# Half-width matmuls in a blocked triangular inverse, and an attention bias table written and read in small parts

## The chip, the cores and the metric

The kernel runs on one core of one Trainium2 chip. The metric is the device time of one execution in microseconds (us), lower is better. Beside the runs' times there is one execution recorded by the hardware profiler; all durations below come from that one.

## What is computed

Eleven stages work one after the other on a state of 256 tokens by 1024 columns: an RWKV-7 mixer, a gated embedding, a differential attention, a second gated embedding, a norm, a feed-forward, a Mamba-2 mixer, two more feed-forwards, a sliding attention, and a fourth feed-forward. Only two of them matter here. The RWKV mixer runs, per head, a recurrence over the tokens:

```python
def step(state, inp):
    r_t, w_t, k_t, v_t, kk_t, b_t = inp
    sa = jnp.einsum('bhij,bhj->bhi', state, kk_t)
    state = (state * w_t[:, :, None, :] - sa[..., None] * b_t[:, :, None, :]
             + v_t[..., None] * k_t[:, :, None, :])
    return state, jnp.einsum('bhij,bhj->bhi', state, r_t)
```

and the sliding attention adds to its scores a bias that depends on head and distance alone:

```python
dist = qi - kj                        # 128 queries, 256 keys
in_window = (dist >= 0) & (dist < 128)
bias = rel_bias[t5_bucket(dist)]      # 32 buckets x 16 heads
s = einsum('bqkrd,bskd->bkrqs', qk, kk) * scale + bias
s = jnp.where(in_window & ..., s, -inf)
```

A feed-forward is `h + 0.5 * ((silu(u @ w1) * (u @ w3)) @ w2)` with `u` the normed state, 1024 columns in and 2816 between.

## The kernel before, in words

**Weights.** Every large weight matrix is streamed in pieces of 512 KB (`wload`, L337). A piece is loaded by a DMA on SyncE's queue (SP) into a tile `wr` (L346), ScalarE (ACT) rounds it to the matmul's four-byte format into `wh` (L350, through the helper at L223), VectorE (DVE) writes the rounding's rest into `wl` (L351, through L198), and TensorE (PE) multiplies with both (L226). DMAs on SP go out in the order of its rows; each waits until its slot of `wr` has been read. In a feed-forward a block of 256 columns (`blocks`, in `ffn` at L510) takes four pieces, two of w1 and two of w3; there are eleven blocks, then the second half's 22 pieces with w2 (`halves`).

**The inverse levels.** The RWKV recurrence is solved in two chunks `t` of 128 tokens for four groups `g` of four heads. For each of these eight (t, g), `scores` (L800) needs the inverse of a unit triangular 128 x 128 matrix per head. It is built by doubling: in half precision, `xt` holds the inverse of the diagonal blocks of size b, `xx` its transpose, `dt` the matrix. A level `lv` from 1 to 6 (b = 2 to 64) joins blocks of size b to blocks of 2b with three products of 128 x 128 per head, four heads in one PSUM bank of 512 columns: `ps` = dt times xx, DVE multiplies it with the level's mask `lev[:, lv]` into `mp` (L849, tile tag `h`), then `pa` = mp times xt and `pb` = xt times mp, which ACT copies into a new `xt` and a new `xx`. A mask has ones on the diagonal too, so the old blocks come through the product. The last level has no `pb`, and ACT writes `X`, the inverse in the four-byte format, for `solve`. That is 12 matmuls per level and chain at levels 1 to 5, 8 at level 6; with the transposition ahead of the levels (4 matmuls, L841) 72 a chain. All `t16` tiles share 14 slots under the tag `h`.

**What sets the order.** The code is written as generators that `weave` advances in turn: four streams `stream(g)` start at steps 0, 9, 24 and 33 (`ST`), and within one the second chunk's `scores` starts five steps after the first's (`SH`). A level takes two steps (two `yield`). Beside them run the gate projections, the bias vector, the embedding's projections and the first output pieces. On top of that a tile scheduler reorders instructions within each engine and chooses the number of slots of a tag where it has room (the numbers in the code are its start); an instruction under `late` keeps its place.

**The bias.** `bias_vec` (L1361) runs within the RWKV stage: one matmul of the table `rel_bias` (33 rows with one for the window, 16 heads) with a one-hot matrix gives a vector of 384 values per head, and one DMA writes it 16 times over into `scr` in DRAM. At the end of the third feed-forward (`ffn10`), `load_bias` (L1376) reads it back with eight DMAs on GpSimd's queue (POOL), each 16 partitions wide, shifted by one element per query, which gives the table `bias`, 128 queries x 16 heads x 256 keys. The sliding attention that follows adds it to its scores.

Of the kernel before, what the change touches and what calls it, by code (L numbers as in the profile page):

```python
# [18 lines left out]
P = 128  # L19
# [20 lines left out]
def constants():  # L40
# [9 lines left out]
    for lv in range(7):  # L50
        b = 1 << lv
        m = (row // (2 * b) == col // (2 * b)) & (row // b % 2 == 0) & (col // b % 2 == 1)
        c[:, C_LEV + lv * P:C_LEV + (lv + 1) * P] = (m if lv == 0 else m.T) | (row == col)
# [32 lines left out]
def take(gen, n):  # L86
    for _ in range(n):
        next(gen)
        yield
# [52 lines left out]
class Net:  # L142
# [367 lines left out]
    def ffn(self, i, j, nxt, kv=False):  # L510
# [114 lines left out]
    def rwkv(self, nxt):  # L625
# [20 lines left out]
        lev = self.m([P, 8, P], F16, tag="lev", bufs=1)  # L646
        self.G.dma_start(lev[:, :7], self.cdram[:, C_LEV:C_LEV + 7 * P].rearrange("p (a b) -> p a b", a=7))
        i16 = lev[:, 7]
# [152 lines left out]
        def scores(t, g):  # L801
# [25 lines left out]
            dt, xt, xx = self.t16(), self.t16(), self.t16()  # L827
            self.add(v4(dt[:]), G[:, 0], bc4(self.ident))
            self.mul(v4(xt[:]), v4(dt[:]), bc4(lev[:, 0]))
# [12 lines left out]
            self.act(xx[:], ps[:])  # L842
            yield
            for lv in range(1, 7):
                ps = self.pq()
                for q in hs:
                    self.mm(ps[:, q], dt[:, q], xx[:, q])
                mp = self.t16()
                self.mul(v4(mp[:]), v4(ps[:]), bc4(lev[:, lv]))  # L849
                yield  # L850
                pa = self.pq()
                for q in hs:
                    self.mm(pa[:, q], mp[:, q], xt[:, q])
                if lv < 6:
                    pb = self.pq()
                    for q in hs:
                        self.mm(pb[:, q], xt[:, q], mp[:, q])
                    xt, xx = self.t16(), self.t16()
                    if True:
                        self.act(xt[:], pa[:])  # L860
                    else:
                        self.V.tensor_copy(xt[:], pa[:])
# [98 lines left out]
        self.V.tensor_copy(i16, self.ident)  # L961
# [623 lines left out]
```

## Time and profile before

| | |
|---|---|
| median of 3 runs | 1540.28 us (1538.38 to 1541.55) |
| profiled execution | 1541.87 us, its span 1540.1 us |
| mean granted PE clock | 0.995 of full speed |
| PE busy with matmuls | 1488.0 us, 97% of the span |
| PE busy with weight loads (beside matmuls) | 1260.3 us, 82% |
| DVE | 1134.3 us, 74% |
| ACT | 874.3 us, 57% |
| POOL | 80.3 us, 5% |
| moved by DMA | 246.98 MB, mean 160 GB/s |

The profiled execution is the one that the views of the trace describe; it took 1.6 us longer than the median. A busy share is a mean over all stages. In the views, a form as `128*128 128x512 f32` is the weights' size and the moved operand's; `LDWEIGHTS` (under PEld) is the load of weights into PE's array that stands ahead of each matmul. A duration of one matmul reaches from its start to its result's end, and matmuls overlap; how fast they follow is seen from starts or from a group's whole length.

### The profile page before, as it was taken

What the parts mean: (1) busy time and instruction counts of PE and PEld (TensorE: products, weight loads), DVE (VectorE), ACT (ScalarE), POOL (GpSimd) and SP (SyncE); (2) the same over time, 40 slices, a digit from 0 to 9 for tenths busy, and PEclk for the clock granted to TensorE, in tenths of its full rate; (3) what the DMA queues carried; (4) which work ended last, traced back from release to release, by engine and by line L of the source; (5) the groups of instructions that cost most, each with busy time, mean ns of one, the idle gap of its engine ahead of it and who ended that gap; (6) DMA issues with size and microseconds to landing.
All of it is one profiled execution on the core that took longest, in us unless ns stands there. A gap on an engine that the chain in (4) does not pass through costs nothing.

```text
span 1540.1 us, 23304 instructions
## 1 busy us (share of the span) xinstructions
PE 1488.0 (97%) x8756; PEld 1260.3 (82%) x8756; DVE 1134.3 (74%) x1958; ACT 874.3 (57%) x1534; POOL 80.3 (5%) x86
## 2 busy tenths in 40 slices
PE   4999999999999999999999999999999999999998
PEld 4988988777778888887887888888878887788887
DVE  6887887776687877559877678865868647777763
ACT  3546556464567655547666655554655545765552
POOL 0000001111201000000001000000100002000000
PEclk9999999999999999999999999999999999999999
DMA  7422333565446666555352656664796653356653
GB/s 210 140 81 59 90 91 131 191 198 154 151 136 193 199 188 190 190 180 149 112 151 84 216 156 189 191 215 140 171 240 191 208 189 110 96 172 185 188 181 109
DMA packets 185716, 246.98 MB, mean 160 GB/s; under 512 B 11017, under 2 KB 124713, under 8 KB 185604
## 3 DMA queue, kind: packets, MB, share of 16 engines
q1 hardware_dynamic: 179124, 233.87, 49.8%
q0 software_dynamic: 2720, 8.05, 2.3%
q10 hardware_dynamic: 3760, 3.58, 1.0%
q8 instruction: 69, 1.13, 0.3%
q14 instruction: 43, 0.35, 0.1%
HBM read 242.16 MB, written 3.54 MB: 160 GB/s over the span
## 4 chain that ended last, share of the span: by engine, by line
PE 84%; DVE 7%; DMA 3%; ACT 3%; POOL 2%; issue 1%; POOLq 0%; ACTq 0%; DVEq 0%
PE pl L226 69%; PE ps L226 12%; PE ps L229 3%; DVE wl L198 2%; DVE s L198 1%; DMA wr<-in_ffn_w_dram 1%; POOL m L234 1%; ACT s L223 1%; DVE s L210 1%; ACT wh L223 1%; DMA wa<-in_rw_a_dram 1%; POOL s L1015 1%; DMA wr<-in_rw_w_in_dram 1%; DVE ac L210 1%; ACT e L223 0%
## 5 line engine op out<-in xcount | busy, mean ns | idle before, releaser
L226 PE MATMUL pl<-wh,s 128*128 128x512 f32 (+1 forms) x2336 | 680.6, 370 | 1.1 <-ACT s L223 1.1
L198 DVE TENSOR_TENSOR wl<-wr,wh 128x1024 fp32r<-128x1024 f32 (+1 forms) x444 | 535.0, 1212 | 154.1 <-ACT wh L223 153.2
L223 ACT ACTIVATE wh<-wr 128x1024 fp32r<-128x1024 f32 (+1 forms) x444 | 458.2, 1043 | 125.6 <-PE pl L226 96.4
L226 PEld LDWEIGHTS pl<-wh,s 128*128 128x128 f32 x2336 | 423.4, 190 | 69.8 <-issue 3.0
L226 PE MATMUL pl<-s,wh 128*128 128x512 f32 x1344 | 472.1, 397 | 3.4 <-ACT wh L223 2.3
L226 PE MATMUL pl<-wl,s 128*128 128x512 f32 (+1 forms) x1168 | 430.6, 369 | 3.1 <-DVE wl L198 3.1
L226 PE MATMUL pl<-s,wl 128*128 128x256 f32 x1344 | 373.9, 279 | 1.3 <-DVE wl L198 1.3
L226 PEld LDWEIGHTS pl<-s,wh 128*128 128x128 f32 x1344 | 252.7, 188 | 63.3 <-ACT wh L223 2.6
L226 PEld LDWEIGHTS pl<-s,wl 128*128 128x128 f32 x1344 | 253.6, 189 | 2.5 <-DVE wl L198 1.8
L226 PEld LDWEIGHTS pl<-wl,s 128*128 128x128 f32 x1168 | 221.9, 190 | 37.8 <-DVE wl L198 4.7
L223 ACT ACTIVATE s<-pl 128x256 f32<-128x256 f32 (+1 forms) x184 | 73.3, 403 | 106.6 <-PE pl L226 102.0
L223 ACT ACTIVATE s<-s 128x512 fp32r<-128x512 f32 (+2 forms) x97 | 61.2, 631 | 87.3 <-DVE s L198 86.7
L198 DVE TENSOR_TENSOR s<-pl,s 128x256 f32<-128x256 f32 x168 | 70.3, 421 | 45.4 <-ACT s L223 45.3
L234 POOL TENSOR_TENSOR m<-m,base 128x2 f32<-128x2 f32 (+2 forms) x25 | 25.2, 1010 | 956.6 <-DVE m L215 934.9
L198 DVE TENSOR_TENSOR s<-s,s 128x512 fp32r<-128x512 f32 (+2 forms) x97 | 66.4, 685 | 1.5
L223 ACT ACTIVATE h<-ps 128x512 f16<-128x512 f32 x88 | 48.3, 600 | 32.8 <-PE ps L226 29.5
L223 ACT ACTIVATE s<-ps,base 128x256 fp32r<-128x256 f32 (+1 forms) x104 | 46.4, 471 | 32.3 <-DVE s L210 17.0
L223 ACT ACTIVATE junk<-H 128x512 bf16<-128x512 f32 x40 | 25.1, 627 | 45.3 <-DVE H L210 28.9
L210 DVE SCALAR_TENSOR_TENSOR s<-ps,base,s 128x256 fp32r<-128x256 f32 x96 | 43.9, 479 | 7.8 <-ACT s L223 7.0
L210 DVE SCALAR_TENSOR_TENSOR H<-pl,m,H 128x512 f32<-128x512 f32 x16 | 12.0, 751 | 47.1 <-PE pl L226 47.1
L226 PE MATMUL ps<-h,h 128*128 128x128 f16 x544 | 44.4, 220 | 2.1 <-ACT h L223 1.9
L210 DVE SCALAR_TENSOR_TENSOR s<-s,s 128x512 f32<-128x512 f32 x56 | 38.4, 686 | 10.6 <-ACT s L223 10.5
(235 smaller groups left out, 1385.8 us busy)
## 6 DMA issues: line engine op xcount, KB each, us to landing
wr<-in_ffn_w_dram SPq DMA_DIRECT2D x264, 512.0 KB, 4.1
wr<-in_ssm_w_in_dram SPq DMA_DIRECT2D x40, 512.0 KB, 4.6
wr<-in_rw_w_in_dram SPq DMA_DIRECT2D x32, 512.0 KB, 3.9
wr<-in_da_w_in_dram SPq DMA_DIRECT2D x32, 512.0 KB, 4.4
wr<-in_pe_w_gate_dram SPq DMA_DIRECT2D x16, 512.0 KB, 6.2
wr<-in_ssm_w_out_dram SPq DMA_DIRECT2D x16, 512.0 KB, 3.7
wr<-in_rw_w_out_dram SPq DMA_DIRECT2D x8, 512.0 KB, 6.5
wr<-in_da_w_out_dram SPq DMA_DIRECT2D x8, 512.0 KB, 6.8
```

Source lines behind the costliest of these rows:

```text
L198: return self.V.tensor_tensor(out=out, in0=a, in1=b, op=op)
L210: self.V.scalar_tensor_tensor(out=out, in0=a, scalar=sc, in1=b, op0=op0, op1=op1, **k)
L223: return self.A.activation(out, a, f, **k)
L226: self.T.matmul(out, l, r, start=start, stop=stop)
L229: self.T.transpose(out, a, self.ident)
L234: self.G.tensor_tensor(out=out, in0=out, in1=self.mhalf[:, :out.free_size()].rearrange("p (a b) -> p a b", a=out.shape[1]) if len(out.shap ...
L1015: self.G.tensor_tensor(out=a[:], in0=a[:], in1=b[:], op=ALU.add)
```

## The change

**Levels.** The masks of a level touch only the off-diagonal part: of the 128 columns of a head, `ps` matters in the 64 whose block is even, `pa` changes the 64 whose block is odd, `pb` the 64 that are even. So each product now moves 64 columns of a head in place of 128, cut out of the old tiles by the view `part(ap, lv, odd)`, whose 64 columns are blocks of b elements with b between. The four heads' 64 columns lie together in 256 columns of PSUM; `pa` and `pb` share one bank. `xt` and `xx` are updated in place: ACT writes only the changed 64 columns a head. `dt`, `xt` and `xx` of a chain are now one tile `inv` (four slots). The mask product goes into one fixed tile per level, `MP[lv]`, six tiles inside `lev`, which grows from 8 to 29 blocks of 128 columns; their other columns hold the identity for good, written once near the start by six POOL copies. The last level copies the unchanged half of `X` too, one ACT operation more. The masks in DRAM shrink to 64 columns for levels 1 to 6, so `lev`'s load is 4 blocks in place of 7.

**Bias.** `bias_vec` runs in the first feed-forward (`ffn00`). Its matmul gives 128 rows (each head eight times over) in place of 16, and `scr` holds each head 128 times in place of 16: eight DMAs on SP of 2 x 128 rows of 1.5 KB (384 KB), one per block from the third block on. `load_bias` in `ffn10` is eight DMAs on SP, each all 128 partitions of two heads (256 KB), one per block from the third on.

```diff
+        if lv == 0:
+            c[:, C_LEV:C_LEV + P] = m | (row == col)
+        else:
+            c[:, C_LEV + P + (lv - 1) * 64:C_LEV + P + lv * 64] = (m.T | (row == col))[:, i // b % 2 == 0]
...
+        bias = self.load_bias() if kv else self.bias_vec() if not (i or j) else iter(())
         for n0 in range(256, 2816, 256):
             l1, l3 = blocks(n0)
-            weave(chain(l1, l3), side) if n0 == 256 else weave(chain(l1, l3))
-        if kv:
-            self.load_bias()
+            weave(chain(l1, l3), side if n0 == 256 else spread(1, 6, take(bias, 1)))
+        weave(bias)
...
-        lev = self.m([P, 8, P], F16, tag="lev", bufs=1)
+        lev = self.m([P, 29, P], F16, tag="lev", bufs=1)
...
+        MP = {lv: lev[:, 1 + 4 * lv:5 + 4 * lv].rearrange("p a b -> p (a b)") for lv in range(1, 7)}
+        def part(ap, lv, odd):
+            return ap.rearrange("p (n two b) -> p n two b", two=2, b=1 << lv)[:, :, odd]
...
-            dt, xt, xx = self.t16(), self.t16(), self.t16()
+            three = self.m([P, 3, 512], F16, "inv", 4)
+            dt, xt, xx = three[:, 0], three[:, 1], three[:, 2]
...
             for lv in range(1, 7):
+                n, b = 256 >> lv, 1 << lv
+                c4 = lambda ap: ap.rearrange("p (n b) -> p n b", n=n)
+                cut = lambda x, q, odd: part(x, lv, odd)[:, q * n // 4:(q + 1) * n // 4]
                 ps = self.pq()
-                for q in hs:
-                    self.mm(ps[:, q], dt[:, q], xx[:, q])
-                mp = self.t16()
-                self.mul(v4(mp[:]), v4(ps[:]), bc4(lev[:, lv]))
+                for q in range(4):
+                    self.mm(ps[:, q * 64:(q + 1) * 64], dt[:, hs[q]], cut(xx, q, 0))
+                mp = MP[lv]
+                self.mul(h4(part(mp, lv, 0)), h4(c4(ps[:, :256])), levc[:, lv - 1]...broadcast_to([P, 4, n // 4, b]))
                 yield
                 pa = self.pq()
-                for q in hs:
-                    self.mm(pa[:, q], mp[:, q], xt[:, q])
+                for q in range(4):
+                    self.mm(pa[:, q * 64:(q + 1) * 64], mp[:, hs[q]], cut(xt, q, 1))
                 if lv < 6:
-                    pb = self.pq()
-                    for q in hs:
-                        self.mm(pb[:, q], xt[:, q], mp[:, q])
-                    xt, xx = self.t16(), self.t16()
-                        self.act(xt[:], pa[:])
-                    self.act(xx[:], pb[:])
+                    for q in range(4):
+                        self.mm(pa[:, 256 + q * 64:256 + (q + 1) * 64], xt[:, hs[q]], cut(mp, q, 0))
+                    self.act(part(xt, lv, 1), c4(pa[:, :256]))
+                    self.act(part(xx, lv, 0), c4(pa[:, 256:]))
                 else:
                     x = XT[t, g] = self.m([P, 512], F32R, "XT", 4)
-                    self.act(x[:], pa[:])
+                    self.act(part(x[:], lv, 0), part(xt, lv, 0))
+                    self.act(part(x[:], lv, 1), c4(pa[:, :256]))
...
+        for mp in MP.values():
+            self.late(self.G.tensor_copy(mp..., i16.unsqueeze(1).broadcast_to([P, 4, P])))
...
-              after(FP, chain(self.bias_vec(), self.ple_proj(0), self.ple_proj(1))), ...
+              after(FP, chain(self.ple_proj(0), self.ple_proj(1))), ...
...
     def bias_vec(self):
-        self.mm(ps[:16, :384], lh, oh[:33, :384])
-        self.scr = self.dp.tile([16, 16, 384], F32, tag="scr", name="scr")
-        self.G.dma_start(self.scr[:], vec[:16, :384].unsqueeze(1).broadcast_to([16, 16, 384]))
-        yield
+        self.mm(ps[:, :384], lh[:33, :P], oh[:33, :384])
+        self.scr = self.dp.tile([16, P, 384], F32, tag="scr", name="scr")
+        scr = self.scr[:].rearrange("h (c j) n -> (h c) j n", j=16)
+        for q in range(0, 16, 2):
+            yield
+            self.late(self.nc.sync.dma_start(scr[:, q:q + 2], vec[:, :384].unsqueeze(1).broadcast_to([P, 2, 384])))
...
     def load_bias(self):
-        for q in range(0, P, 16):
-            self.late(self.G.dma_start(self.bias[q:q + 16], ... ap=[[383, 16], [384 * 16, 16], [1, 256]]))
+        for h in range(0, 16, n):
+            yield
+            self.late(self.nc.sync.dma_start(self.bias[:, h:h + n], ... ap=[[383, P], [384 * P, n], [1, 256]]))
```

In the levels PE has as many instructions as before, and they are narrower. In the middle of a burst of level products on PE stood before (`h` are the half-precision tiles, `ps` a PSUM bank):

```order
L226 LDWEIGHTS h_983
L226 MATMUL ps_1011<-h_937,h_983 128x128
L226 LDWEIGHTS h_937
L226 MATMUL ps_1016<-h_983,h_937 128x128
L226 LDWEIGHTS h_937
```

and now stand (`inv` is a chain's tile of three, `lev` the tile with the masks and mask products):

```order
L231 LDWEIGHTS lev_95
L231 MATMUL ps_1014<-inv_942,lev_95 128x64
L231 LDWEIGHTS inv_942
L231 MATMUL ps_1014<-lev_95,inv_942 128x64
L231 LDWEIGHTS inv_942
```

The moved operand is 64 columns wide, each matmul still has its own load of weights, and both products go to one bank.

On SP in the first feed-forward a row of weight loads stood before:

```order
L346 DMA wr_6106<-in_ffn_w_2_dram 128x4x256
L346 DMA wr_6128<-in_ffn_w_2_dram 128x4x256
L346 DMA wr_6163<-in_ffn_w_2_dram 128x4x256
L346 DMA wr_6185<-in_ffn_w_2_dram 128x4x256
L346 DMA wr_6217<-in_ffn_w_2_dram 128x4x256
```

and now the writes of the bias vector stand between them:

```order
L351 DMA wr_5960<-in_ffn_w_2_dram 128x4x256
L1395 DMA scr<-s_5783 128x2x384
L351 DMA wr_5995<-in_ffn_w_2_dram 128x4x256
L1395 DMA scr<-s_5783 128x2x384
L351 DMA wr_6018<-in_ffn_w_2_dram 128x4x256
L351 DMA wr_6050<-in_ffn_w_2_dram 128x4x256
L351 DMA wr_6072<-in_ffn_w_2_dram 128x4x256
L351 DMA wr_6107<-in_ffn_w_2_dram 128x4x256
L1395 DMA scr<-s_5783 128x2x384
```

One write goes out ahead of about every fourth weight load from there on.

The bias table was read by eight rows on POOL, after the last of the third feed-forward's norm operations there:

```order
L234 TENSOR_TENSOR m_11485<-m_11485,base_72 128x2
L234 TENSOR_TENSOR m_11498<-m_11498,base_72 128x2
L1380 DMA bias<-scr 16x16x256 x8
L234 TENSOR_TENSOR m_13043<-m_13043,base_72 128x2
L1406 TENSOR_TENSOR m_13057<-m_13057,base_72 128x8 x2
```

and now by eight on SP, among that stage's weight loads:

```order
L351 DMA wr_11532<-in_ffn_w_2_dram 128x4x256
L1403 DMA bias<-scr 128x2x256
L351 DMA wr_11555<-in_ffn_w_2_dram 128x4x256
L351 DMA wr_11587<-in_ffn_w_2_dram 128x4x256
L351 DMA wr_11609<-in_ffn_w_2_dram 128x4x256
L351 DMA wr_11644<-in_ffn_w_2_dram 128x4x256
L1403 DMA bias<-scr 128x2x256
```

A read of two heads goes out ahead of about every fourth weight load, and the row with all eight is gone from POOL.

The built programs also differ in the slots of the weight tiles, of which the diff says nothing: `wr`, `wh` and `wl` lie at 6, 8 and 6 addresses before and at 3 each now. `wload`'s own numbers (3 and 3) are unchanged.

## Rows read from the trace of the kernel before

**Rows 1.** Page, busy time of each engine over the span (share), x instructions.

```profile
PE 1488.0 (97%) x8756; PEld 1260.3 (82%) x8756; DVE 1134.3 (74%) x1958; ACT 874.3 (57%) x1534; POOL 80.3 (5%) x86
```

**Rows 2.** Stretches (us): PE, PEld, DVE, ACT, POOL busy (instructions), granted clock, DMA share, GB/s.

```profile
100.00:250.00 150.00, 147.01 (x1423) 131.30 (x1422) 121.85 (x238) 86.80 (x158) 10.44 (x11) 1.00 0.30 84
500.00:640.00 140.00, 140.00 (x779) 121.34 (x778) 109.57 (x150) 82.62 (x124) 0.69 (x1) 1.00 0.66 197
```

**Rows 3.** Tile h (levels), duration ns min/median/max, first and last start us, forms.

```profile
L226 PE MATMUL ps<-h,h x544: 216/219/234, 100.3 to 274.3; 128*128 128x128 f16 x182
L226 PEld LDWEIGHTS <-h x576: 95/98/153, 99.2 to 274.3; 128*128 128x128 f16 x192
L223 ACT ACTIVATE h<-ps x88: 581/597/641, 99.6 to 265.8; 128x512 f16<-128x512 f32 x88
L198 DVE TENSOR_TENSOR h<-ps,lev x48: 672/683/693, 100.9 to 273.0; 128x512 f16<-128x512 f32 x48
```

**Rows 4.** Timeline, inverse levels: start us, us, engine line op tiles xcount [idle before <-releaser].

```profile
169.55 0.61 PE L226 MATMUL ps<-h,h 128*128 128x128 f16 x8
223.65 0.11 PEld L226 LDWEIGHTS <-h 128*128 128x128 f16 x2 [1.00 <-DVE h L198]
178.28 1.00 PE L226 MATMUL ps<-sa,GB 128*128 128x64 f32 x8
```

**Rows 5.** Tile bias, landing of its eight reads; waits 1095 to 1140 us: total, times, longest.

```profile
DMA to landing us min/median/max: 8.2/13.8/18.7
ACT wh L223 <- DMA wr<-in_ffn_w_dram: 9.2, 1, 9.2
```

**Rows 6.** Third feed-forward: PE's timeline, then the stretch 1125 to 1135 us.

```profile
1128.06 0.49 PE L226 MATMUL pl<-s,wh 128*128 128x512 f32 x1 [2.25 <-ACT wh L223]
1129.32 0.39 PE L226 MATMUL pl<-s,wl 128*128 128x256 f32 x1 [0.76 <-DVE wl L198]
...
1129.96 0.63 PE L226 MATMUL pl<-s,wh 128*128 128x512 f32 x1
...
1130.60 0.63 PE L226 MATMUL pl<-s,wh 128*128 128x512 f32 x1
...
1133.54 0.40 PE L226 MATMUL pl<-s,wh 128*128 128x512 f32 x1
...
1133.89 0.39 PE L226 MATMUL pl<-s,wh 128*128 128x512 f32 x1
...
1125.00:1135.00 10.00, 6.98 (x30) 5.56 (x30) 6.92 (x10) 6.64 (x11) 0.00 (x0) 0.83 1.10 336
```

**Rows 7.** Page, costliest groups, 256 columns out of PSUM: busy, mean ns | idle before, releaser.

```profile
L223 ACT ACTIVATE s<-pl 128x256 f32<-128x256 f32 (+1 forms) x184 | 73.3, 403 | 106.6 <-PE pl L226 102.0
L198 DVE TENSOR_TENSOR s<-pl,s 128x256 f32<-128x256 f32 x168 | 70.3, 421 | 45.4 <-ACT s L223 45.3
```

**Rows 8.** POOL's copies' neighbours: a group of lines; waits 20 to 100 us.

```profile
L1015 POOL TENSOR_TENSOR s<-s,s 128x512 f32<-128x512 f32 x8 | 14.0, 1756 | 51.5 <-DVE s L198 47.6 <-PE ps L229 3.9
POOL s L283 <- PE pl L226: 40.9, 1, 40.9
PE ps L226 <- DMA wa<-in_rw_a_dram: 5.6, 1, 5.6
```

**Rows 9.** Timeline of PE: the bias vector's matmul.

```profile
218.00 0.81 PE L226 MATMUL ps<-s,s 33*16 33x384 f32 x2
```

**Rows 10.** First feed-forward: one weight load's timeline; issues 500 to 640 us, median us to landing.

```profile
575.27 0.37 SPq L346 DMA_DIRECT2D wr<-in_ffn_w_dram  x1
588.77 1.05 ACT L223 ACTIVATE wh<-wr 128x1024 fp32r<-128x1024 f32 x1
590.67 1.22 DVE L198 TENSOR_TENSOR wl<-wr,wh 128x1024 fp32r<-128x1024 f32 x1
591.91 0.37 SPq L346 DMA_DIRECT2D wr<-in_ffn_w_dram  x1
wr<-in_ffn_w_dram SPq DMA_DIRECT2D x53, 512.0 KB, 4.4
```

More of the change, by code (lines that the diff above doesn't have):

```diff
@@ L87, in take @@
     for _ in range(n):
-        next(gen)
+        if next(gen, gen) is gen:
+            return
         yield
@@ L826, in scores @@
                 yield
-            dt, xt, xx = self.t16(), self.t16(), self.t16()
-            self.add(v4(dt[:]), G[:, 0], bc4(self.ident))
-            self.mul(v4(xt[:]), v4(dt[:]), bc4(lev[:, 0]))
+            three = self.m([P, 3, 512], F16, "inv", 4)
+            dt, xt, xx = three[:, 0], three[:, 1], three[:, 2]
+            self.add(v4(dt), G[:, 0], bc4(self.ident))
+            self.mul(v4(xt), v4(dt), bc4(lev[:, 0]))
             pv = self.pq()
@@ L961, in rwkv @@
         self.V.tensor_copy(i16, self.ident)
+        for mp in MP.values():
+            self.late(self.G.tensor_copy(mp.rearrange("p (h c) -> p h c", h=4), i16.unsqueeze(1).broadcast_to([P, 4, P])))
         weave(chain(*[value(g) for g in range(4)]), chain(lora(), mix(1, *xk), mix(0, *xr)))
@@ L973, in rwkv @@
         weave(after(FH, residual()), after(FG[0], spaced(FG[1], *[gate(g) for g in range(4)])),
-              after(FP, chain(self.bias_vec(), self.ple_proj(0), self.ple_proj(1))), when(done(OP[0]), after(OP[1], chain(take(l0, OP[2]), take(l1, OP[3])))),
+              after(FP, chain(self.ple_proj(0), self.ple_proj(1))), when(done(OP[0]), after(OP[1], chain(take(l0, OP[2]), take(l1, OP[3])))),
               *[after(n, stream(g)) for g, n in enumerate(ST)])
@@ L1361, in bias_vec @@
     def bias_vec(self):
[L1363 to L1365 removed]
+        l0, lh = self.s(), self.s()
+        self.late(self.V.memset(lh[:33, :P], 1.0))
+        self.G.dma_start(l0[:32, :16], self.I["rel_bias_2"])
+        self.V.tensor_copy(lh[:32, :P].rearrange("p (h c) -> p h c", c=8), l0[:32, :16].unsqueeze(2).broadcast_to([32, 16, 8]))
         oh = self.s()
[L1367 removed]
+        self.late(self.G.dma_start(oh[:33, :384], self.cdram[:33, C_OH:C_OH + 384]))
         ps = self.pq()
[L1369 removed]
+        self.mm(ps[:, :384], lh[:33, :P], oh[:33, :384])
         vec = self.s()
[L1371 to L1381 removed]
+        self.V.tensor_copy(vec[:, :384], ps[:, :384])
+        self.scr = self.dp.tile([16, P, 384], F32, tag="scr", name="scr")
[3 more added lines that the diff above has]
+            self.late(self.nc.sync.dma_start(scr[:, q:q + 2], vec[:, :384].unsqueeze(1).broadcast_to([P, 2, 384])))
+    def load_bias(self):
+        self.bias, n = self.cp.tile([P, 16, 256], F32, tag="bias", name="bias"), 2
+        for h in range(0, 16, n):
+            yield
+            a = self.scr[h]
+            self.late(self.nc.sync.dma_start(self.bias[:, h:h + n], bass.AP(tensor=a.tensor, offset=a.offset + 127,
+                                                                           ap=[[383, P], [384 * P, n], [1, 256]])))
     def swa(self, nxt):
@@ L1518, in run @@
             weave(self.ple_proj(0), self.ple_proj(1))
-            weave(self.bias_vec())
             if "diff" not in stages:
```

22 lines of the change are left out of this document (7 added, 15 removed).

## The prediction

> **What bounds the kernel now.** I read the busy table first: the reader is to see that TensorE (PE) is busy 97% of the span [rows 1], so time is to be had only where PE waits, where its clock is low, or where it has less to do. The stretches come next: from 100 to 250 us, where the inverse levels run, PE is busy 147.01 of 150 us at full clock, DVE 121.85 and ACT 86.80; in the first feed-forward, 500 to 640 us, PE is busy all 140.00 us and the DMA engines 0.66 of the time [rows 2]. So in the inverse stage the bound is PE's own work, with 3.0 us of waits; in the feed-forward it is PE alone. Third, the tile view of the levels, for what is halved [rows 3]; fourth, the timeline at single bursts, for how closely half-precision matmuls follow each other [rows 4]. Fifth, the waits and the timeline of the third feed-forward, the one stretch where a DMA stops PE [rows 5, 6].
>
> **Term 1, the levels on PE.** The count stays: 544 half-precision matmuls, each with its weight load [rows 3]. Each streams 64 columns where it streamed 128. Eight of them in a row take 0.61 us and one takes 0.219, so they start (0.61 - 0.22) / 7 = 56 ns apart [rows 3, 4]. No row has a half-precision matmul of 64 columns. From below: half the columns, half the distance, 28 ns. From above: nothing is gained, 56 ns, because each still loads 128 columns of weights; the row that speaks for this has four-byte weights and 64 columns, eight in 1.00 us, over 100 ns apart however few the columns [rows 4]. But the half-precision load is another thing: after a wait, two of them take 0.11 us together where one takes 0.098, so the second began within 15 ns of the first [rows 3, 4]. A load that lets the next begin after 15 ns is hidden behind 28 ns of columns. I take 30 ns: 544 x 26 = 14.1 us less PE work; bounds 0 and 15.2.
>
> A rule of the Trainium skill speaks against this term. Its page TensorE: Matmul & The Clock Gate, section LDWEIGHTS, prices a weight load by its columns, 128 / 1.2 GHz or 107 ns, and its section on the back-to-back gap gives about 81 ns for a pair with 128 columns; by that price halving the moved columns would give nothing. The rows with 56 ns a pair disagree with both figures.
>
> How much of it arrives? PE runs in order, so what a step of the inverse waits for must be covered by other PE work. That cover shrinks by 12 x 26 ns = 0.3 us per level and chain, with two or three chains interleaved. The wait shrinks as well: DVE's product from 683 to about 421 ns, each of two ACT evacuations from 597 to about 403, the durations of the same engines on 256 columns out of PSUM [rows 3, 7]: 0.26 + 0.39 = 0.65 us per level. About even, so I keep the 3.0 us of waits and add 2 for places where the cover was thin: **-12 us**. DVE and ACT lose 48 x 0.26 = 12.6 and 80 x 0.19 = 15 us of work, worth nothing by themselves, as neither is the bound. The extra copy of the last level on ACT, eight of about 0.4 us, ends in front of a chain's solve and is inside the 2 us. The mask products now go into one tile per level in place of a fresh one, so a second chain at the same level would wait; chains start five steps or more apart and a level is two steps, so I give it nothing (0 to +3).
>
> **Term 2, the copies at the start.** Six copies of identities on POOL. The nearest row is a POOL operation of 512 four-byte columns, 1.76 us, so at most 10.5 us; POOL then sat idle for 40.9 us, and PE itself waits 5.6 us there for its first small weights, wa [rows 8]. The copies stand behind the issue of those weights on POOL. Nothing; without that cover it would delay the column loads behind them, needed much later.
>
> **Term 3, the bias vector.** Its matmul, 0.81 us on PE [rows 9], leaves the inverse stage and comes back in the first feed-forward, where PE is as full: zero, 0.8 us either way. Its two small loads are issued by POOL, which is idle in that stretch, well before the matmul's place, so PE does not wait for them.
>
> **Term 4, the bias table.** Before, eight reads of 256 KB come at once on POOL's queue and take 8.2 to 18.7 us to land; in that time a weight load is late and ACT waits 9.2 us for it [rows 5]. PE's share of this is 2.25 + 0.76 us of waits, and then a stretch at the lower clock: over 1125 to 1135 us the granted clock is 0.83 of 2.4 GHz, which is (1 - 0.83) x 10 / 0.5 = 3.4 us at 1.2 GHz, behind those waits [rows 6]. The pairs of matmuls at 1129.96 and 1130.60 start 0.64 us apart, those at 1133.54 and 1133.89, back at 2.4 GHz, 0.35 [rows 6], so 3.4 x (1 - 0.35 / 0.64) = 1.5 us of it are lost. Spread over eight blocks of 11 us, a read of 256 KB stands before every fourth weight load; a weight load is twice that and is taken in 2.77 us at a DMA share of 0.66 [rows 2, 10], 1.8 us of DMA time, so a read costs 0.9. The share goes to about 0.74. PE is not stopped: **-4.5 us** (bounds 0 and -4.5).
>
> **Term 5, the writes.** Eight writes of 384 KB on SP's queue in the first feed-forward, each in front of every fourth weight load: 384 / 512 x 1.8 = 1.4 us each, share to about 0.78. The weights land 4.4 us after their issue [rows 10]. They hide if the weights are early enough. If that cover were gone, 8 x 1.4 = 11 us here and 8 x 0.9 = 7 in the third feed-forward would show.
>
> **Term 6, the weights' slots.** This the diff does not say. In the built program the three weight tiles lie at 3 addresses each, before at 6, 8 and 6. The row of a load issued at 575.27 and of its low half's end, 590.67 + 1.22 = 591.89, with the next issue into that slot at 591.91, shows six loads in flight, 16.6 us or 2.77 us each [rows 10]. With three slots a load must land, be rounded by ACT and be subtracted by DVE within 3 x 2.77 = 8.3 us. It needs 4.4 + 1.05 + 1.22 = 6.7 [rows 10]; in turn, with the evacuations between on ACT and DVE, the span from ACT's start at 588.77 to 591.89 is 3.1, which makes 7.5. So it fits, with 0.8 to 1.6 us to spare, and a slot comes free two loads, 5.5 us, before PE's next turn at it, of which 2.3 to 3.1 go to ACT and DVE: what is ready stands 2.4 to 3.2 us before PE wants it. A write of 1.4 us in front of every fourth load fits into the two together. But at stage borders, where ACT and DVE are held up, less is in stock. From bounds 0 and +6 (twelve borders at half a microsecond) I take **+2 us**.
>
> **Sum.** -12 - 4.5 + 2 = -14.5 us. The profiled execution took 1541.87 us, 1540.1 of it its span: 1527.4. The median of the runs, 1540.28, is 1.6 us lower than that execution; carried over, **1526 us**. A measurement of this kernel can tell about 0.2%, 3.1 us, from no change.
>
> **Rivals.**
> - **The weight load bounds the half-size matmul.** Pairs stay near 56 ns. For it: the four-byte row. Against it: the 15 ns. Then term 1 keeps only what shorter evacuations give to the 3.0 us of waits, say 1.5: -1.5 - 4.5 + 2 = -4, 1536. The page's load price ends here too. Chance 0.12.
> - **The chains become the bound.** PE's work shrinks but its in-order waits on DVE, ACT and the shared mask tiles grow: of 14 us 4 arrive, 1534. For it: PE already waits 3.0 us there, and work memory has become tighter for other tiles too. Against it: the wait shrinks with the cover. Chance 0.12.
> - **Slower: three slots are the bound.** Issue to the end of the low half takes more than 8.3 us; from that point on every load of the feed-forwards is paced by it. At 8.7 us a load takes 2.90 in place of 2.77 us, and 264 of them give +34 us: 1560. For it: 0.8 us to spare is little, and the transfers now stand between. Against it: the landing of 4.4 us was measured with six in flight, with fewer it is hardly longer. Chance 0.08.
> - **The transfers show.** The slots hold, but a load behind a write or read is late to PE: +11 to +18, most of the gain, 1541. Chance 0.06.
>
> **How the numbers follow.** The forecast keeps 0.62 and the predicted time is its own. Its own range is 1517 (all 15.2, no waits, -4.5, nothing for the slots) to 1532. With the first two rivals the range goes to 1538; what is left out above is 0.14, below a little. Faster by over 0.2% means under 1537.2: the forecast, the chains, and most of the first rival (its 1536 lies near the border): 0.82. The rest of that rival and the transfers make 0.10, the slots 0.08.
>
> **What would show it.** Right: half-precision matmuls of 64 columns about 30 ns apart; PE's waits from 100 to 240 us near 5 us; the first projection's start after the inverse some 12 us earlier; no wait and no stretch at 1.2 GHz in the third feed-forward; PE busy throughout the first one. In the slots, the distance from issue to the low half's end falls from 16.6 to 8.3 us. Wrong: a pair still at 56 ns; PE waiting for wh or wl inside a feed-forward; a stage after the inverse that takes longer than before by more than a microsecond or two.

## The result and the profile after

The changed kernel takes 1528.62 us (median of 13 runs, 1524.03 to 1536.37) where the kernel before, on the same chip, takes 1539.48 (13 runs): ratio 0.993, 95% interval 0.9913 to 0.9947, 10.9 us faster (8 to 13). The prediction was 1526, within 1517 to 1538, which is 14.3 us less than the 1540.28 it started from (ratio 0.9907). That ratio lies just outside the interval here and inside that of a later measurement on another chip (0.9883 to 0.9925). The recorded execution of the changed kernel takes 1528.67 us, its span 1526.9, 13.2 less than before's.

What answers to [rows 1], the page of the changed kernel:

```profile
PE 1474.7 (97%) x8756; PEld 1246.5 (82%) x8756; DVE 1125.5 (74%) x1959; ACT 859.7 (56%) x1542; POOL 80.6 (5%) x83
```

PE has lost 13.3 us of busy time and its share is the same, so over the whole span it waits as long as before (52 us). To [rows 3] answer these, from the views of the tiles `lev` and `inv` (min/median/max in ns, first and last start, forms):

```profile
L231 PE MATMUL ps<-inv,lev x192: 191/193/207, 103.2 to 259.6; 128*128 128x64 f16 x192
L203 DVE TENSOR_TENSOR lev<-ps,lev x48: 408/418/426, 102.0 to 258.5; 128x256 f16<-128x256 f32 x48
...
L228 ACT ACTIVATE inv<-ps x88: 365/385/629, 100.8 to 250.9; 128x256 f16<-128x256 f32 x80, 128x512 f16<-128x512 f32 x8
```

and to the bursts of [rows 4] these rows of PE's timeline (start us, us, engine, line, operation, tiles, count):

```profile
140.19 0.28 PE L231 MATMUL ps<-inv,lev 128*128 128x64 f16 x4
140.30 0.28 PE L231 MATMUL ps<-lev,inv 128*128 128x64 f16 x4
140.42 0.28 PE L231 MATMUL ps<-inv,lev 128*128 128x64 f16 x4
```

A group of four starts every 0.11 to 0.12 us, so the matmuls are 29 ns apart, against 56 before. In the stretches of [rows 2], and in the third feed-forward while the bias table is read (columns as there):

```profile
100.00:236.00 136.00, 132.81 (x1423) 120.02 (x1424) 110.96 (x238) 73.23 (x164) 8.81 (x8) 1.00 0.29 86
500.00:640.00 140.00, 140.00 (x758) 120.73 (x758) 102.87 (x137) 76.71 (x116) 0.00 (x0) 1.00 0.68 212
1095.00:1185.00 90.00, 89.88 (x521) 78.43 (x520) 72.70 (x103) 51.48 (x82) 1.54 (x1) 1.00 0.69 214
```

The first row is the same number of matmuls as in [rows 2] (1423) in 14 us less, with 3.2 us of waits where there were 3.0. The second is the first feed-forward with its writes, and PE does not wait. In the third row the waits of [rows 6] are gone. The weight load of [rows 10] is now, again in the first feed-forward:

```profile
566.44 0.37 SPq L351 DMA_DIRECT2D wr<-in_ffn_w_dram  x1
572.41 1.06 ACT L228 ACTIVATE wh<-wr 128x1024 fp32r<-128x1024 f32 x1 [1.44 <-issue]
573.50 1.23 DVE L203 TENSOR_TENSOR wl<-wr,wh 128x1024 fp32r<-128x1024 f32 x1 [0.48 <-ACT wh L228]
```

From issue to the low half's end it takes 574.73 - 566.44 = 8.3 us, three loads of 2.77 us, where it was 16.6.

To see where the time went, count PE's matmuls from the last one back: most are the same work in each kernel. The table has the time between the same marks (the 8300th, 6500th, 5500th, 4450th, 3560th, 2400th, 2000th and 960th from the end); in brackets what PE sat idle and how long it ran at 1.2 GHz, both in us. "Again" is a second recorded execution of the changed kernel; the last three are experiments that follow.

| stretch | before | after | after, again | levels alone | wide, spread | levels, tight |
|---|---|---|---|---|---|---|
| start to the levels | 88.4 (21.8, 6.8) | 89.5 (21.8, 0) | 88.2 (21.2, 0) | 88.2 (20.3, 0) | 86.6 (20.1, 6.8) | 87.8 (20.9, 0) |
| levels to the end of the inverse | 203.8 (7.8, 0) | 186.4 (6.7, 0) | 187.5 (7.8, 0) | 187.5 (7.2, 0) | 190.3 (7.0, 6.8) | 191.7 (8.1, 7.8) |
| first embedding to second | 210.0 (5.9, 3.4) | 212.4 (9.0, 0) | 211.4 (8.2, 0) | 209.4 (5.8, 3.4) | 210.6 (5.8, 6.8) | 213.5 (7.8, 5.9) |
| first feed-forward | 198.5 (0, 0) | 199.3 (0, 0) | 199.2 (0, 0) | 198.5 (0, 0) | 198.5 (0, 0) | 198.5 (0, 0) |
| Mamba-2 | 161.1 (4.0, 0) | 164.8 (4.3, 6.8) | 161.7 (4.3, 0) | 164.1 (3.8, 6.8) | 162.5 (3.9, 3.4) | 164.5 (3.9, 6.8) |
| second feed-forward, start of third | 220.0 (1.1, 0) | 222.6 (1.1, 0) | 220.3 (1.1, 0) | 219.9 (1.1, 0) | 220.0 (1.1, 0) | 222.6 (1.1, 0) |
| third, around the table's reads | 74.6 (4.3, 3.4) | 69.8 (1.8, 0) | 72.3 (2.0, 3.4) | 73.5 (3.2, 3.4) | 70.0 (1.3, 0) | 82.7 (11.7, 10.2) |
| rest of it, sliding attention | 196.0 (2.5, 0) | 196.6 (2.8, 0) | 197.7 (2.8, 0) | 197.2 (2.5, 0) | 197.2 (2.5, 0) | 197.6 (2.7, 0) |
| fourth feed-forward | 183.1 (0.5, 0) | 181.0 (0.7, 0) | 181.0 (0.7, 0) | 180.9 (0.5, 0) | 180.8 (0.5, 0) | 181.0 (0.7, 0) |

So in the first recorded execution the inverse levels gave 17.4 us, the table 4.8 and the fourth feed-forward 2.1. What went was 1.1 ahead of the levels, 2.4 at the borders after the inverse, 0.8 in the first feed-forward, 3.7 in the Mamba-2 stage, 2.6 in the second feed-forward and 0.6 in the rest.

### The profile page after: what moved, and what is told of

The parts are those of the page before. It is cut to its first block, busy times and chain, and to the rows that moved or that the text cites. A ratio compares the mean times of both kernels' runs of the same rounds, so it can differ in the third digit from the quotient of the medians.

```text
span 1526.9 us, 23363 instructions
## 1 busy us (share of the span) xinstructions
PE 1474.7 (97%) x8756; PEld 1246.5 (82%) x8756; DVE 1125.5 (74%) x1959; ACT 859.7 (56%) x1542; POOL 80.6 (5%) x83
## 4 chain that ended last, share of the span: by engine, by line
PE 82%; DVE 8%; ACT 3%; issue 2%; DMA 2%; POOL 2%; ACTq 0%; POOLq 0%; DVEq 0%
PE pl L231 68%; PE ps L231 11%; PE ps L234 3%; DVE wl L203 2%; DVE s L203 1%; ACT wh L228 1%; DVE s L215 1%; POOL s L1032 1%; POOL m L239 1%; ACT e L228 1%; ACT s L228 1%; DVE b L203 0%; DMA wr<-in_pe_w_gate_dram 0%; DMA wr<-in_rw_w_in_dram 0%; POOL m L1429 0%
## 5 line engine op out<-in xcount | busy, mean ns | idle before, releaser
L203 DVE TENSOR_TENSOR wl<-wr,wh 128x1024 fp32r<-128x1024 f32 (+1 forms) x444 | 536.6, 1210 | 280.7 <-ACT wh L228 279.6
L228 ACT ACTIVATE wh<-wr 128x1024 fp32r<-128x1024 f32 (+1 forms) x444 | 465.4, 1048 | 463.4 <-PE pl L231 306.2
L228 ACT ACTIVATE inv<-ps 128x256 f16<-128x256 f32 (+1 forms) x88 | 31.0, 406 | 27.0 <-PE ps L231 26.8
L234 PE MATMUL ps<-base,s 128*128 128x128 f32 x200 | 32.3, 276 | 9.5 <-POOL s L1032 4.2
L234 PEld LDWEIGHTS ps<-base,s 128*128 128x128 f32 x200 | 23.8, 143 | 17.0 <-POOL s L1032 6.7
L231 PEld LDWEIGHTS ps<-s,e 128*128 128x128 f32 x240 | 31.9, 195 | 4.9 <-DVE e L203 2.5
```

The source lines that it names most:

```text
L203: return self.V.tensor_tensor(out=out, in0=a, in1=b, op=op)
L228: return self.A.activation(out, a, f, **k)
L231: self.T.matmul(out, l, r, start=start, stop=stop)
L234: self.T.transpose(out, a, self.ident)
```

## The experiments

The medians of one chip belong together; the kernel before took 1543.5 to 1546.2 us on those used here, so kernels of different chips are compared by their ratio to it. The diffs are cut; dots stand for what is left out.

**The levels alone** (bias as before).

```diff
-              after(FP, chain(self.ple_proj(0), self.ple_proj(1))), ...
+              after(FP, chain(self.bias_vec(), self.ple_proj(0), self.ple_proj(1))), ...
...
+        if kv:
+            self.load_bias()
```

> Only the levels are changed; the bias is written and read as before. In the built program the weight tiles keep 6, 9 and 7 addresses. Theory: PE's shorter matmuls carry the change, 544 x 27 ns = 14.4 us, less what the start and the clock take back, so 8 to 13 us faster than before (ratio 0.9915 to 0.995), and the third feed-forward still shows the wait of about 2 to 3 us and the stretch at 1.2 GHz. Rival, the gain of the whole change comes mostly from the bias table: under 5 us faster. If three addresses for the weights cost something in the whole change, this kernel's feed-forwards run quicker than those of the whole change.

Measured: 1524.4 us, ratio 0.9862 (0.9837 to 0.9887), 20.7 us faster. Twice more, on other chips, it took 1521.79, ratio 0.9847 (0.9822 to 0.9872), and 1526.94, ratio 0.9881 (0.9858 to 0.9903). That is more than the 8 to 13 us forecast, and the levels alone give at least as much as the whole change. In the program the weight tiles keep 6, 9 and 7 addresses: it is the two parts together that make memory scarce.

**The bias alone.**

```diff
+        bias = self.load_bias() if kv else self.bias_vec() if not (i or j) else iter(())
...
+            weave(chain(l1, l3), side if n0 == 256 else spread(1, 6, take(bias, 1)))
```

> Only the bias is changed; the levels are those of before. Weight tiles at 6, 8 and 6 addresses. Theory: the reads spread over eight blocks no longer stop PE, 4 to 5 us faster (ratio about 0.997), and no wait of ACT for a weight load in the third feed-forward; the matmul of the bias vector costs as much as it saves. Rival, the stall only moves: a weight load behind a write or a read is late and PE waits in the first or third feed-forward, within 1 us of before.

Measured: 1533.76 us, ratio 0.9924 (0.9897 to 0.995): 11.3 us faster, more than forecast. Its recorded execution is 7.8 us shorter than before's; 5.5 of it are in the third feed-forward, where the waits behind the reads are gone, and 2.2 are PE's pace in the fourth (below). The runs of before on this chip had a mean granted clock of 0.9941, these 0.9967; by an estimate from these two, (0.9967 - 0.9941) x 1540 = 4 us go with the clock. What the rest is stays open. The two parts alone gave 20.7 and 11.3 us on this chip, and the whole change (with its copies moved, next) 16.5: they do not add up.

**The copies of the identities moved from 18 to about 60 us.**

```diff
-        for mp in MP.values():
-            self.late(self.G.tensor_copy(...))
         weave(chain(*[value(g) for g in range(4)]), chain(lora(), mix(1, *xk), mix(0, *xr)))
...
         self.load_vec()
+        for mp in MP.values():
+            self.late(self.G.tensor_copy(...))
```

> The whole change, with the six POOL copies of identities issued after POOL's first column loads, at about 60 us, instead of at 18 us. Theory: at 18 to 25 us the copies stretch DVE's operations beside them by 0.41 us each (1.62 in place of 1.21 us for a low half) and PE's first projection ends 1.0 us later than before; moved, the first 8700 matmuls from the end start 1 us earlier and the run is 1 us faster than the whole change, too little for the interval but plain in the trace. Rival, the start's delay is the weight DMA's or the clock's and stays: no difference in the trace at 33 us.

Measured: 1528.58 us, ratio 0.9887 (0.986 to 0.9913), the time of the whole change. The theory got no support: the stretch to the levels took 87.5 us here (6.8 of it at 1.2 GHz), 88.4 before without any copies, and 86.6 to 89.5 in the other recorded executions with the copies near 18 us (the doubled matmuls and the two addresses, both below, aside). PE's first transpositions start anywhere between 14.40 and 17.11 us in these executions, so a microsecond cannot be told from that. At their new place, 59.68 to 65.30 us, the copies lengthen some of DVE's operations as they did at the old one (last section).

**Each narrow matmul issued twice.**

```diff
-                    self.mm(pa[:, q * 64:(q + 1) * 64], mp[:, hs[q]], cut(xt, q, 1))
+                    for _ in range(2):
+                        self.mm(pa[:, q * 64:(q + 1) * 64], mp[:, hs[q]], cut(xt, q, 1))
... the same at the products into ps and into the other half of pa
```

> The whole change, each of the 544 narrow matmuls issued twice into the same place (the second overwrites the first with the same values). Same PE work as with 128 columns, while DVE and ACT keep their half-size operations and the waits stay. Theory, PE's own work is the bound in the inverse: 544 x 29 ns = 15.8 us slower than the whole change, near 1544. Rival, the chains of waits between PE, DVE and ACT are the bound: the second matmul fills waits, under 8 us slower.

Measured: 1539.78 us, ratio 0.9971 (0.9949 to 0.9992), 11.2 above the kernel with the moved copies on the same chip. PE's busy time in the levels' stretch is the first row here, the changed kernel's the second:

```profile
100.00:270.00 170.00, 167.42 (x2149) 152.96 (x2149) 124.65 (x261) 85.64 (x190) 12.15 (x12) 1.00 0.28 85
```

```profile
100.00:255.00 155.00, 150.96 (x1606) 136.84 (x1607) 124.64 (x264) 84.42 (x189) 12.15 (x12) 1.00 0.31 91
```

With nearly the same DVE and ACT work, 543 more matmuls take 15 us more, and PE waits 2.6 us in place of 4.0. In the recorded executions the end of the inverse comes at 290.7 us against 275.7 to 278.1 in the two of the changed kernel and the one with moved copies: 12.6 to 15.0 of the 15.8 us arrive. By the medians it is 11.2, or 70%. Both are above the rival's 8: PE's own work is the bound there.

**The whole change and the levels alone on one chip.** No edit.

> The whole change once more, unaltered, beside the levels alone on the same chip. Theory: with the weight tiles at 3 addresses the borders after the inverse (gated embedding, differential attention) idle about 3 us more than with 6, 9 and 7, and the matmul of the bias vector costs 0.7 us in the first feed-forward, which together eat what the spread reads give: 2 to 5 us slower than the levels alone. Rival, the levels alone only had luck with the clock and with PE's pace: within 1 us of each other. The stretches at 1.2 GHz and the pace in each feed-forward (346.5 or 353.5 ns a pair) differ from the earlier recorded execution of this same kernel.

> The levels alone once more, unaltered, so that it stands beside the whole change on the same chip. Theory and rival as for the whole change; near 1524, and PE's idle time after the inverse and before the first feed-forward is again about 6 us against 9 of the whole change.

Measured: 1529.33 us, ratio 0.9904 (0.9883 to 0.9925), against 1521.79: 7.5 us, and the intervals do not meet. The idle time from the inverse to the first feed-forward is 8.2 against 5.8 us, as expected, and the vector's matmul with its place in the first feed-forward costs 0.7; at the later borders 0.5, 0.3 and 0.2 more. That is 4.1 of the 7.5. Where the rest comes from is not shown: the two recorded executions are equally long, as that of the levels alone ran 13.6 us at 1.2 GHz and the other 3.4.

**The levels, and the old narrow table's reads spread.**

```diff
         for q in range(0, P, 16):
-            self.late(self.G.dma_start(self.bias[q:q + 16], ...
+            yield
+            self.late(self.nc.sync.dma_start(self.bias[q:q + 16], ...
```

> The levels, and of the bias only the spreading: the table's eight reads go out on SP, one per block of the third feed-forward, from the small table of before; the vector's matmul stays in the inverse stage, where it was. Weight tiles at 6, 9 and 7 addresses. Theory: it keeps the gain of the levels and takes away the 2.1 us of waits in the third feed-forward without the price of the three addresses and without the matmul's 0.7 us: 2 to 4 us faster than the levels alone, 5 to 8 faster than the whole change. Rival, the waits come back elsewhere or the gain of spreading was luck with the clock: within 1 us of the levels alone.

Measured: 1532.54 us, ratio 0.9925 (0.9906 to 0.9945), 10.7 slower than the levels alone: both theory and rival fall. PE's waits in the third feed-forward (total, times, longest):

```profile
PE pl L231 <- DVE wl L203: 3.7, 7, 0.5
PE pl L231 <- ACT wh L228: 3.6, 7, 0.6
```

Behind nearly every read PE waits half a microsecond for `wh` and again for `wl`, 7.3 us in all; the recorded execution is 7.7 us longer than that of the levels alone. Spreading does not help this form; the whole change reads the same 2 MB, one read a block, without a wait. What differs is the form, 16 partitions a read or 128, and the weight tiles' addresses; the wide table below settles which.

**Two addresses for each weight tile in place of three.**

```diff
+W0 = 2, 2
...
-        nr, nh = WB.get(self.at, (3, 3))
+        nr, nh = WB.get(self.at, W0)
```

> The whole change with two addresses for each of the weight tiles in place of three. Theory: a slot is then free again only after two loads, 5.5 us, and needs 6.7 to 8.1 us, so every load of a feed-forward is paced by its own turn, at least 3.35 us in place of 2.72 for each of 444: 200 us or more slower than the whole change, and PE waits for wh and wl throughout. Rival, the three slots already had room to spare and two suffice: under 50 us slower.

Measured: 1714.21 us in a single run, 185 above the whole change on the same chip: far from the rival, a little under the size forecast. In the first feed-forward PE is busy 72.37 us of 80:

```profile
520.00:600.00 80.00, 72.37 (x384) 56.95 (x383) 57.05 (x90) 43.41 (x74) 2.44 (x4) 1.00 0.58 167
```

Three is the smallest number that holds the pace; four and five were not tried.

**The levels with the wide table,** spread on SP and at once on POOL.

```diff
-        self.scr = self.dp.tile([16, 16, 384], F32, tag="scr", name="scr")
-        self.G.dma_start(self.scr[:], vec[:16, :384].unsqueeze(1).broadcast_to([16, 16, 384]))
+        self.scr = self.dp.tile([16, P, 384], F32, tag="scr", name="scr")
+        self.G.dma_start(scr[:], vec[:, :384].unsqueeze(1).broadcast_to([P, 16, 384]))
...
-        for q in range(0, P, 16):
+        for h in range(0, 16, n):
-            self.late(self.G.dma_start(self.bias[q:q + 16], ... ap=[[383, 16], [384 * 16, 16], [1, 256]]))
+            self.late(self.G.dma_start(self.bias[:, h:h + n], ... ap=[[383, P], [384 * P, n], [1, 256]]))
```

> The levels and the wide table of the whole change (128 copies of each head, reads of 128 partitions x 2 heads), spread over eight blocks on SP; the vector's matmul stays in the inverse stage and its write is one transfer of 3 MB on POOL's queue there. Weight tiles at 6, 9 and 7 addresses. Only the table's form differs from the levels with the narrow spread reads. Theory: it is the form that matters, reads into 16 partitions hold up the weights and reads into 128 do not: no waits of 0.5 us behind each read, 1518 to 1523, 9 us or more faster than with the narrow spread reads, and 1 to 3 us faster than the levels alone. Rival, the distance between reads and loads on SP's queue is to blame, or the slots: as slow as the narrow spread reads, near 1532.

> The levels and the wide table, but all eight reads at once on POOL's queue after the last block is issued, as before. Only the table's form differs from the levels alone. If the form matters: the weight load behind the reads is late by less than before, ACT's wait shrinks from about 9 us and PE waits under 1 us in the third feed-forward (2.1 us with the levels alone). If spreading matters: the 2 MB still crowd the weights, PE waits 2 us or more. In time both lie within 3 us of the levels alone; the trace decides.

> The levels alone, unaltered, as the mark for the two kernels with the wide table on the same chip: 1521 to 1525, PE's waits in the third feed-forward 2 us.

Measured: 1523.25 us spread, ratio 0.9868 (0.9848 to 0.9887); 1522.89 at once, 0.9871 (0.9848 to 0.9893); the levels alone 1526.94, 0.9881. Against the narrow reads spread (0.9925) the intervals do not meet: with the same spreading the wide form is about 0.6%, some 9 us, faster. Among themselves the three can't be told apart in time; in the trace they can. In neither with the wide table does PE wait from 1085 to 1210 us. The two sets of rows are 1085 to 1120 us in 40 slices, eight reads at once, first in the wide form, then in the narrow one of the levels alone (GB/s in each slice, and POOL's queue: packets, MB, share of the 16 DMA engines):

```profile
GB/s 197 154 358 62 0 0 13 118 372 144 163 394 391 357 328 338 369 351 351 341 335 343 351 339 349 352 342 352 328 270 332 69 80 238 306 82 332 187 8 158
q0 software_dynamic: 640, 2.10, 17.2%
```

```profile
GB/s 0 0 63 295 265 94 218 268 131 124 193 116 139 164 109 153 121 201 149 139 170 126 202 152 138 159 117 138 249 240 305 349 350 348 348 350 344 351 324 356
q0 software_dynamic: 640, 2.10, 40.3%
```

The same 2.10 MB hold the DMA engines 2.3 times as long in the narrow form. For most of that time all traffic together gets 109 to 202 GB/s, in the wide form 328 to 394. The waits of the levels alone, in that execution ACT's and then PE's:

```profile
ACT wh L228 <- DMA wr<-in_ffn_w_dram: 11.2, 1, 11.2
```

```profile
PE pl L231 <- ACT wh L228: 4.4, 1, 4.4
```

In the wide form ACT does not wait for a weight load at all. The form matters, the spreading does not, as far as the weights have 6, 9 and 7 addresses; at once with three was not tried.

Which side of the form matters was not varied by itself, but the code leaves little choice. On the DRAM side one read is alike in both: 256 rows of 1 KB out of 384 KB that lie together. The destination differs: 16 rows into each of 16 partitions, or 2 into each of 128. What is left on the DRAM side is that all eight narrow reads go over the same 384 KB; spread, they do so about 11 us apart, and behind seven of them PE still waited.

**The levels alone with scarce memory.** On PE, DVE and SP the instructions and their order are those of the levels alone, and ACT has as many; only addresses differ.

```diff
+        self.pad = self.c([P, 2048], F32, "pad")
+        self.G.memset(self.pad[:, 0:1], 0.0)
...
+        self.G.tensor_copy(self.pad[:, 1:2], self.pad[:, 0:1])
```

> The levels alone, with 8 KB of each partition's work memory held by a tile that is otherwise not used (one element written at the start and copied at the end). In the built program the weight tiles then lie at 3 addresses each, XT at 2 and sa at 5, nearly as in the whole change, in place of 6, 9 and 7, 7 and 34. Nothing else differs from the levels alone. Theory: it is the scarcer memory that makes PE idle about 2 us more in the gated embedding and 0.6 us in the differential attention and second embedding, with 0.3 us each at the later borders, 3 us in all: PE's idle time between the inverse and the first feed-forward rises from 5.8 to over 8 us, and the run is 2 to 4 us slower than the levels alone (1524 to 1531). Rival, the waits at these borders come from the moved bias vector or its transfers: the idle time there stays at 5.8 us. The feed-forwards themselves keep their time in either case.

Measured: 1544.25 us, ratio 1.000 (0.9981 to 1.0019): the whole gain of the levels is gone. The idle time after the inverse is 7.8 us against 5.8, so most of what the whole change loses there (8.2 and 9.0) comes of the memory. What the theory missed is the third feed-forward:

```profile
PE pl L231 <- ACT wh L228: 8.7, 1, 8.7
PE pl L231 <- DVE wl L203: 0.9, 2, 0.5
```

With three addresses the reads of the narrow table stop PE for 9.6 us, with more of them for about 2 to 5, and behind that wait come 10.2 us at 1.2 GHz. The weight load is late by the same time in both: ACT waits 11.0 us for it here at the longest, 11.2 in the levels alone of the experiment before. What differs is the addresses, and with them how much ready weight can stand before PE meanwhile. By the table this stretch makes 9.2 of the 20.8 us between the two recorded executions; 4.2 are in the inverse stage, which ran 7.8 us at 1.2 GHz, 4.1 at the borders after it, and 2.7 are PE's pace in the second feed-forward. The clock and the pace differ between executions of one kernel too, so the 1.4% is not the addresses' price alone: the mean granted clock of these runs is 0.991, that of the levels alone 0.995.

## Why the prediction came out as it did

**Levels (-12 forecast).** The mechanism was right and the size too small. The pitch came out as 29 ns against the 30 taken; by the two recorded executions the stretch became 16.3 to 17.4 us shorter, 0.75 of it the vector's matmul that left. Counted from each matmul's start to the next, where PE was not idle between, the narrow products took 13 us less (14.1 taken), and 2.2 us came from the four-byte matmuls among them, which stood in no term; why these follow each other closer was not found. The step that failed is "add 2 for places where the cover was thin": the waits did not grow (7.8 before, 6.7 and 7.8 after). That fits DVE's product at 418 ns and ACT's copies at 385, as the rows of the same engines had said (421 and 403), but no run varied them. The page TensorE: Matmul & The Clock Gate of the Trainium skill prices a load at 107 ns in its section LDWEIGHTS; a single load does last 98 ns in this trace, but as a price in a row of such matmuls the trace speaks against it: a load with its matmul follows the pair before after 29 ns. The same page's formula for the gap of single matmuls, N / 2.4 + 2.5 ns in the section Back-to-back issue gap, gives 29.2 for 64 columns and 55.8 for 128, and both agree.

**Copies (0) and vector (0).** Held as far as the runs can tell: moving the copies changed neither the time nor the stretch to the levels beyond what executions differ by, and the vector's matmul left 0.75 us and took 0.7.

**Table (-4.5).** The size was near by luck: 4.8 us in the first recorded execution of the changed kernel, 2.3 in the second, which ran 3.4 us at 1.2 GHz there, and 5.5 in the bias alone. The reason was wrong. Term 4 put the stall to eight reads that "come at once on POOL's queue", so that spreading them would end it. Spread, reads into 16 partitions made the kernel 10.7 us slower; at once, reads into 128 stopped nothing. The price of "a read costs 0.9" I took by bytes from a weight load, which writes 128 partitions; by the rows for eight reads at once, 17.2 and 40.3% of 35 us, a wide read holds the engines for 0.75 us and a narrow one for 1.8. The gain came because the change also made the reads wide, which the term did not weigh. The Trainium skill, page SBUF — State Buffer, section Door 1: The DMA port swizzle, says that a transfer's bandwidth depends on how many of 16 ports its partitions reach; by its table 16 neighbours reach four. The rows above agree in kind, 109 to 202 GB/s against 328 to 394.

**Writes (0).** Held: from the 5300th to the 4450th matmul from the end 164.06 us before and 164.14 after.

**Slots (+2).** The steady state came as worked out, 8.3 us a turn; that the low half is then ready some 3 us before PE is worked out the same way and stands in no row. The cost came at the borders, 2.3 to 3.1 us after the inverse and about 1 later, 3 to 4 where 2 were taken; the tight kernel shows 2.0 and 0.5 of it with the addresses alone. The rival "three slots are the bound" did not happen, and its point lies just beyond: at two the loads set the pace. But the term was summed as if it stood alone, and the tight kernel shows that it hangs together with the table's: the same late weight load cost PE 9.6 us with three addresses and 4.9 with more.

**What was in no term.** The executions differ by clock and pace, up to some 4 us at one place, and the median of the changed kernel (1528.62) lies 2.6 above the forecast. That the sum is this near is in part luck: the levels gave about 4 us more than forecast, and in the first recorded execution the borders, the clock in the Mamba-2 stage and the pace of the second feed-forward took more than that back. By the prediction's own signs, those for right came (29 ns, 3.2 us of waits from 100 to 240 us, 16 us earlier after the inverse, 8.3 us a turn, PE busy throughout the first feed-forward), with a stretch at 1.2 GHz in the third feed-forward in the second execution; and one sign for wrong came too: in the first execution three stages after the inverse took 2.4 to 3.7 us longer.

The levels alone, or with the wide table and the vector left in the inverse stage, beat the kernel before and, it seems, the whole change: ratios of 0.985 to 0.988 against 0.989 to 0.993 for the whole change (0.989 with its copies moved). Between chips these intervals overlap in part. On one chip the levels alone were 7.5 us faster than the whole change, with intervals apart; on another all five of their runs (1523.8 to 1525.4) were shorter than all six of the whole change with its copies moved (1525.7 to 1532.1).

## What to carry to other kernels

Halving the moved columns of half-precision matmuls from 128 to 64 nearly halved their time here (56 to 29 ns), where they were what PE was busy with; below 64 nothing was measured. Price a transfer by the partitions it writes as well as by its bytes: the narrow one slowed everything that shared the DMA engines with it. When a change adds tiles, compare the addresses that the other tiles get before and after: the same instructions on scarcer memory were 1.2 to 1.5% slower here, in part by clock and pace, and the largest loss showed where a slow transfer met a short stock of weights.

## What the runs showed of the hardware

**Two paces of the same stream.** In the feed-forwards' first halves matmuls of 512 and 256 columns alternate, and PE does not wait. Their starts repeat in one of two patterns, 346.7 or 353.3 ns a pair. One of the two holds through a first half, unless a wait of PE changes it, and executions of one kernel differ. The changed kernel in its two recorded executions, the stretch 930 to 960 us of the second feed-forward (PE alone, then all engines; the number in PE's brackets, 172 or 175, is its matmuls):

```profile
930.00:960.00 30.00, 30.00 (x172) 1.00 0.62 192
```

```profile
930.00:960.00 30.00, 30.00 (x175) 26.22 (x174) 23.84 (x33) 17.71 (x28) 0.00 (x0) 1.00 0.67 189
```

A feed-forward's first half takes 2.3 us more at the slower one. It is most of the 2.6 us of the second feed-forward and the 2.1 of the fourth in the table. What chooses the pace was not found; tile addresses are not it, since the two are the same program.

**The clock after a wait.** In the Mamba-2 stage PE waits 2.35 us for DVE, in all executions of the table. Before, the clock stayed at 2.4 GHz; in the changed kernel's first recorded execution 6.8 us at 1.2 GHz followed, in its second none, in the others of the table 3.4 or 6.8. PE's timeline and the stretch behind it, first execution:

```profile
800.31 1.54 PE L231 MATMUL ps<-s,e 128*128 128x64 f32 x6 [2.35 <-DVE e L203]
```

```profile
803.00:806.00 3.00, 3.00 (x13) 1.98 (x11) 1.19 (x3) 1.69 (x6) 0.00 (x0) 0.50 0.51 182
```

In the second row the granted clock is 0.50. The wait is of the same length each time, and what the clock does behind it is not: the stage took 3.7 us more than before in the first execution and 0.6 in the second. So a small effect is read from the segment in which it lies, and from several executions.

**POOL beside DVE.** While POOL ran its six copies of two-byte values (18.26 to 24.91 us in the changed kernel), most of DVE's operations beside them took 0.41 us longer each: 1.62 us against 1.21 for the low half at 19.18, 1.09 against 0.68 for an operation of 510 columns at 20.73, 0.57 against 0.16 for an operation with one input at 21.74. Not all did: the low half at 22.22 took its 1.21.
